# Expert weights of a two-block transformer kernel: one transfer with 8 KB runs for each matrix, in place of two with 4 KB runs

## The chip, the core and the metric

The kernel runs on one core of a Trainium2 chip. The metric is the device time of one execution in microseconds (us). The profile gives the engines the names PE (matrix multiplies), PEld (its weight loads), DVE (vector), ACT (scalar), POOL (GpSimd) and SP (the engine whose queue issues most transfers). A transfer is carried out by 16 DMA engines that all queues share.

## What is computed

Two transformer blocks work on 1024 tokens of width 1024 in float32. The first has an mLSTM and a convolution mixer and then a mixture of 64 experts, of which each token takes 8, plus a shared expert; the second has chunked attention and a state space branch and then 16 experts, of which each token takes 2. The change touches the experts alone. Cut to that, the reference is:

```python
def body(acc, xs):                       # for one block of rows of one expert e
    rows, rw, e = xs
    xb = hpad[rows]
    y = (jax.nn.silu(xb @ we_gate[e]) * (xb @ we_up[e])) @ we_down[e]
    return acc.at[rows].add(y * rw[:, None].astype(y.dtype)), None
...
shared = (jax.nn.silu(hf @ ws_gate) * (hf @ ws_up)) @ ws_down
```

An expert has three float32 matrices of 1 MB: gate and up, 1024 x 256, and down, 256 x 1024. The 80 experts of both blocks have 240 such matrices.

## The kernel before

The class `Moe` serves both blocks. Experts are ordered by their number of tokens and every rank has a fixed capacity (`CAPS1`: 400 down to 64 rows, `CAPS2`: 240 down to 64). A unit is an expert, or half of one with over 256 rows; the units of many rows (over 128) and of few rows alternate.

For each unit, `fetch` gathers the rows of its tokens into `xg` with an indirect transfer from POOL's queue (L1097), `trans` transposes them on PE, and `load` brings the three matrices of the expert with plain transfers from SP's queue (L1132, in `halves`). `split` turns every float32 half matrix into a high and a low part in float32r: ACT copies (L83, `guh`, `wdh`), DVE subtracts (L84, `gul`, `wdl`). PE multiplies three products of parts (`pg` for gate and up, `psy` for down). ACT scales the result into a tile `y` (L1268), of which there are three, and POOL issues an indirect transfer that adds the rows of `y` to `acc` in HBM (L1269, L1220 for experts of 64 rows), up to 128 rows each. I call it the scatter. Scatters of one block of the network add into the same tensor, so the program has each wait until the one before it has landed.

The loop `main` works on three units at once: in pass i it loads and gathers ahead, splits the gate, up and down matrices of unit i + 1, runs the gate and up matmuls of unit i, and the down matmuls and the scatter of unit i - 1. SP's queue keeps the order of the program; the other engines' order is chosen by a scheduler. The split parts have six places of a half matrix for gate and up, and three for down (`wd=3`), which is one and a half experts.

A loaded half matrix lies in a place `raw` of 4 KB per partition. There are eight, 4 MB in all, and a load waits for the split that reads the place's old content; a place that comes free is taken by the next load in SP's order. At the start of the first expert stage three places more are lent from a pool that is closed soon after (`Z = 3`); the shared expert's first matrices and, at the end, seven rows of tokens for the next stage (`head`) use the same places.

```python
    def halves(self, src):
        kc = src.shape[1]
        out = []
        for j in range(2):
            raw = self.tile("raw", [128, kc // 2, 2048 // kc], F32)
            self.k.nc.sync.dma_start(raw, src[:, j * kc // 2:(j + 1) * kc // 2])
            out.append(raw)
        return out
```

Of the kernel before, what the change touches and what calls it, by code (L numbers as in the profile page):

```python
# [7 lines left out]
F32 = mybir.dt.float32  # L8
# [21 lines left out]
class Kern:  # L30
# [793 lines left out]
    def moe1(self, es0, caps, es1, head):  # L824

        nc, I = self.nc, self.I
        dve, act, gp = nc.vector, nc.scalar, nc.gpsimd
        acc = self.acc_d = self.dram.tile([1024, 1024], F32, name="acc1")
        with ExitStack() as es:
            kp = self.pool(es1, "m1k")  # L830
            moe = Moe(self, "m1", 64, caps, I['we_gate'][0], I['we_up'][0], I['we_down'][0], self.h2_d, acc)
            moe.psum(es)
            moe.pools(self.pool(es1, "m1r"), raw=8)
            moe.pools(self.pool(es, "m1a"), gu=4)
            moe.pools(self.pool(es, "m1x"), x=1, sg=2)
            up = moe.shared_up(self.hT, I['ws_gate'][0], I['ws_up'][0], self.chain)

            def fill(n):
                for _ in range(n):
                    next(up, None)  # L840
            fill(FILL[0])
            with ExitStack() as e1, self.tc.manual_schedule(engines={mybir.EngineType.PE}):
                tp = self.pool(e1, "m1t")
                pl = self.logits(moe.pst, "pt")
                S = tp.tile([128, 8, 64], F32, name="S")
                act.activation(S, pl, AF.Sigmoid)
                br = tp.tile([128, 64], F32, name="br")
                b = I['b_router']
                nc.sync.dma_start(br, bass.AP(tensor=b.tensor, offset=b.offset, ap=[[0, 128], [1, 64]]))
                sel = tp.tile([128, 8, 64], F32, name="sel")  # L850
                dve.tensor_tensor(sel, S, br[:, None].to_broadcast([128, 8, 64]), op=OP.add)
                rep = tp.tile([128, 8, 64], F32, name="rep")
                m8 = tp.tile([128, 8, 8], F32, name="m8")
                for c in range(8):
                    dve.max(m8[:, c], sel[:, c])
                    dve.match_replace(rep[:, c], m8[:, c], sel[:, c], -3.0e38)
                mask = tp.tile([128, 8, 64], BF, name="mask")
                dve.tensor_tensor(mask, rep, sel, op=OP.not_equal)
                fill(FILL[1])
                wt = tp.tile([128, 8, 64], F32, name="wt")  # L860

                def gate():
                    dve.tensor_mul(wt, S, mask)
                    sm = tp.tile([128, 8], F32, name="sm")
                    dve.reduce_sum(sm, wt, axis=AX.X)
                    dve.reciprocal(sm, sm)
                    dve.tensor_scalar(sm, sm, 2.5, None, op0=OP.mult)
                    dve.tensor_tensor(wt, wt, sm[:, :, None].to_broadcast([128, 8, 64]), op=OP.mult)
                    return wt
                moe.setup(kp, mask, gate, fill)  # L870
            moe.pools(self.pool(es, "m1b"), xg=4, oh=2, q=2)
            with moe.ordered():
                with ExitStack() as e1:

                    raw = moe.room['raw']
                    moe.pools(self.pool(e1, "m1z"), raw=Z)
                    moe.room['raw'] = raw[:4] + raw[8:] + raw[4:8]
                    moe.start()
                    moe.split(0, 0)
                    moe.room['raw'] = raw[:8]  # L880
                fill(16)
                es0.close()
                mc = self.pool(es, "m1c", side="right")
                moe.pools(mc, gu=2, wd=3, su=2, hh=2, hl=2, y=3)
                moe.pools(self.pool(es, "m1y", side="right"), x=1)
                moe.room['gu'] = [moe.room['gu'][i] for i in GUO]
                moe.shared_down(I['ws_down'][0])
                moe.main()
                head([moe.tile("raw", [128, 4, 256], F32).rearrange("p a b -> p (a b)") for _ in range(7)], moe.pst)

            raw[:] = [(mc, 2, "gu" + n) for n in "hl"]
            moe.room['gu'] = moe.room['gu'][:2]
            moe.overflow()


class Moe:
# [228 lines left out]
        return [self.halves(w[ds(e, 1)].rearrange("o (p c) n -> p (o c) n", p=128)) for w in (self.wg, self.wu, self.wd)]  # L1125

    def halves(self, src):
        kc = src.shape[1]
        out = []
        for j in range(2):  # L1130
            raw = self.tile("raw", [128, kc // 2, 2048 // kc], F32)
            self.k.nc.sync.dma_start(raw, src[:, j * kc // 2:(j + 1) * kc // 2])  # L1132
            out.append(raw)
        return out

    def shared(self, w):

# [144 lines left out]
    def shared_up(self, hT, wg, wu, chain):  # L1282

        nc, behind = self.k.nc, self.k.tc.issue_after
        sq, ad, tr, sc = chain
        part = lambda v: v.rearrange("p a b -> p (a b)").rearrange("p (c n) -> p c n", n=128)
        raw, W = [], []
        for f in range(2):
            for w in (wg, wu):
                raw.append(part(self.tile("raw", [128, 4, 256], F32)))  # L1290
                nc.sync.dma_start(raw[-1], w[:, f * 128:f * 128 + 128].rearrange("(c p) n -> p c n", p=128))
        for j, r in enumerate(raw):
            h, l = (part(self.tile("gu", [128, 4, 256], F32R, "gu" + n)) for n in "hl")
            with behind(sq) if j > 1 else ExitStack(), behind(ad) if j > 1 else ExitStack():
                self.k.split(h, l, r)
            W.append((h, l))
        hs = self.hs = self.tile("x", [128, 2, 2, 1024], F32R)
        n = 0
        for f in range(2):
            for t in range(2):  # L1300
                c = slice(t * 512, t * 512 + 512)
                pg, pu = (self.psg.tile([128, 512], F32, name="pg") for _ in range(2))
                for p, (wh, wl) in zip((pg, pu), W[2 * f:]):
                    for i in range(8):
                        if i % 4 == 0:
                            if n:
                                yield
                            n += 1
                        with behind(sc) if n > 4 else ExitStack():
                            self.k.mm3(p, wh[:, i], wl[:, i], hT[0][:, i, c], hT[1][:, i, c], i == 0, i == 7)  # L1310
                s = self.tile("sg", [128, 512], F32)
                nc.scalar.activation(s, pg, AF.Sigmoid)
                nc.vector.tensor_mul(s, s, pg)
                nc.vector.tensor_mul(s, s, pu)
                self.k.split(hs[:, 0, f, c], hs[:, 1, f, c], s)
        yield
# [414 lines left out]
class Second:  # L1731
# [382 lines left out]
    def experts(self, em, hT, caps):  # L2114
        k, nc, I = self.k, self.k.nc, self.k.I
        dve, act, gp = nc.vector, nc.scalar, nc.gpsimd
        with ExitStack() as es:
            kp = k.pool(es, "m2k", side="right")
            moe = Moe(k, "m2", 16, caps, I['w_e_gate_2'][0], I['w_e_up_2'][0], I['w_e_down_2'][0], self.h3_d, self.acc_d)
            moe.psum(es)  # L2120
            with ExitStack() as e1:
# [4 lines left out]
                for o, n, nm in ((0, 4, 'group_bias_2'), (4, 16, 'expert_bias_2')):  # L2126
                    b = I[nm]
# [12 lines left out]
                e4, oh, p4 = T("e4", [8, 4]), T("goh", [8, 4]), T("p4", [8, 4])  # L2140
# [37 lines left out]
                    return wt.rearrange("p c g e -> p c (g e)")  # L2178
                moe.setup(kp, mask.rearrange("p c g e -> p c (g e)"), gate)
            em.close()  # L2180
            moe.pools(k.pool(es, "m2w"), raw=8, gu=6, wd=3, x=2, xg=4, oh=2, q=2, sg=2, su=2, hh=2, hl=2, y=3)
            with moe.ordered():
                moe.start()
                moe.main()
# [1 line left out]


FILL = 5, 2, 1, 1
Z = 3
GUO = 0, 0, 4, 4, 0, 0  # L2190

CAPS1 = [400] + [256] * 2 + [240] + [224] * 2 + [208] * 2 + [192] * 5 + [176] * 5 + [160] * 5 + [144] * 6 + [128] * 7 + [112] * 10 + [96] * 3 + [80] * 7 + [64] * 8
# [69 lines left out]
```

## Time and profile before

| what | value |
|---|---|
| device time, median of 3 runs | 2698.14 us (2696.0 to 2704.96) |
| device time of the profiled execution | 2692.12 us |
| span of its instructions | 2690.3 us |
| mean granted clock of TensorE | 0.963 of full speed |
| first expert stage | about 602 to 1566 us of the span |
| second expert stage | about 2421 to 2690 us |

The span runs from the first to the last instruction; 1.8 us lie around it. The profiled execution is one execution, 6.0 us below the median of the runs. In the views, "busy" is the time in which an engine executes instructions. A matmul's end is modelled, so a busy PE is not PE at its peak. An idle time is put down to the semaphore that came last by the profile; where the engine it names had long been done, it was another one, often a transfer.

### The profile page before, as it was taken

How to read it: one execution, taken by the hardware profiler on the slowest of the kernel's cores; microseconds unless marked ns; L12 is line 12 of the kernel's file. 1: busy time of each engine (PE TensorE's matmuls, PEld its weight loads, DVE VectorE, ACT ScalarE, POOL GpSimd, SP SyncE). 2: the span in 40 equal slices, each digit the busy share in tenths (PEclk: the TensorE clock that was granted, in tenths of full speed). 3: DMA queues.
4: the chain of work that ended last, by engine and by line, in shares of the span. 5: the costliest groups of instructions: out<-in, count | busy, mean ns of one | idle time of the engine just before them, and what ended most of it. 6: DMA issues, size and time to landing. Idle time of an engine off the chain costs nothing. (4 is left out here: it accounts for less than half of the span.)

```text
span 2690.3 us, 46156 instructions
## 1 busy us (share of the span) xinstructions
PE 2492.9 (93%) x17156; PEld 2127.8 (79%) x17156; DVE 1793.0 (67%) x4037; ACT 1332.8 (50%) x2327; POOL 534.0 (20%) x467
## 2 busy tenths in 40 slices
PE   6999987999999999999999939899999989987996
PEld 4798866987988888888877628688898778976884
DVE  4874788677777788887865453763243876278882
ACT  4322156324677776767765544223222772225773
POOL 0000021311232233233233230230001200002332
PEclk9999998999999999999999969999999999997998
DMA  7111183237899999999999864444311024148995
GB/s 252 33 50 61 44 279 113 103 109 268 244 308 309 312 314 299 307 316 315 301 319 317 252 216 95 123 89 107 114 32 56 1 95 150 56 165 291 320 291 120
DMA packets 259820, 507.52 MB, mean 189 GB/s; under 512 B 68761, under 2 KB 151905, under 8 KB 259592
## 3 DMA queue, kind: packets, MB, share of 16 engines
q1 hardware_dynamic: 231720, 409.36, 45.4%
q0 software_dynamic: 26720, 90.98, 14.9%
q10 hardware_dynamic: 1152, 4.19, 0.4%
q8 instruction: 136, 2.23, 0.3%
q14 instruction: 92, 0.75, 0.1%
HBM read 414.42 MB, written 90.04 MB: 188 GB/s over the span
## 5 line engine op out<-in xcount | busy, mean ns | idle before, releaser
L84 DVE TENSOR_TENSOR gul<-raw,guh 128x1024 fp32r<-128x1024 f32 x288 | 348.4, 1219 | 114.5 <-ACT guh L83 113.4
L83 ACT ACTIVATE guh<-raw 128x1024 fp32r<-128x1024 f32 x288 | 303.1, 1061 | 176.4 <-DMA raw<-in_we_gate_dram 67.8
L1185 PE MATMUL pg<-x,guh 128*128 128x320 f32 (+8 forms) x1248 | 383.7, 371 | 2.6 <-DVE sg L1233 2.6
L1184 PE MATMUL pg<-x,gul 128*128 128x160 f32 (+8 forms) x1092 | 278.1, 256 | 0.0
L1185 PEld LDWEIGHTS pg<-x,guh 128*128 128x128 f32 x1248 | 245.2, 200 | 9.9 <-DVE sg L1233 2.7
L1269 POOL DMA_INDIRECT acc<-y,m1idx x87 | 149.3, 1717 | 492.4 <-DMA acc<-y,m1idx 103.3
L1184 PEld LDWEIGHTS pg<-x,gul 128*128 128x128 f32 x1092 | 219.0, 201 | 3.4 <-issue 0.8
L84 DVE TENSOR_TENSOR wdl<-raw,wdh 128x1024 fp32r<-128x1024 f32 x144 | 175.6, 1222 | 60.9 <-ACT wdh L83 59.3
L88 PE MATMUL psy<-wdh,hh 128*128 128x512 f32 (+8 forms) x444 | 179.2, 405 | 7.4 <-ACT y L1268 7.0
L89 PE MATMUL psy<-wdl,hh 128*128 128x512 f32 (+8 forms) x444 | 175.4, 395 | 0.0
L90 PE MATMUL psy<-wdh,hl 128*128 128x512 f32 (+8 forms) x444 | 169.5, 400 | 0.0
L1097 POOL DMA_INDIRECT xg<-h_d,m1idx x95 | 122.4, 1289 | 180.7 <-PE pt L1119 91.9
L398 DVE SCALAR_TENSOR_TENSOR y<-u,cw,y 128x1024 f32<-128x1024 f32 x120 | 153.9, 1283 | 2.7
L83 ACT ACTIVATE wdh<-raw 128x1024 fp32r<-128x1024 f32 x144 | 151.6, 1054 | 7.3 <-PE psy L90 4.6
L88 PE MATMUL pg<-guh,x 128*112 128x256 f32 (+3 forms) x528 | 152.0, 288 | 1.0 <-ACT x L83 1.0
L1119 PEld LDWEIGHTS pt<-ident,xg 128*128 128x128 f32 (+8 forms) x888 | 119.3, 196 | 40.2 <-issue 18.6
L1119 PE MATMUL pt<-ident,xg 128*128 128x128 f32 (+8 forms) x888 | 134.2, 279 | 17.1 <-DVE x L84 5.3
L89 PE MATMUL pg<-gul,x 128*112 128x256 f32 (+3 forms) x528 | 149.9, 284 | 0.0
L90 PE MATMUL pg<-guh,x 128*112 128x256 f32 (+3 forms) x528 | 149.9, 285 | 0.0
L76 DVE TENSOR_TENSOR wlo<-wraw,whi 128x2048 fp32r<-128x2048 f32 (+2 forms) x37 | 83.3, 2251 | 92.9 <-ACT whi L75 92.8
L89 PE MATMUL pf<-bl,whi 128*128 128x512 f32 (+1 forms) x384 | 140.5, 369 | 3.0 <-DVE bl L1829 2.9
L88 PE MATMUL pf<-bh,whi 128*128 128x512 f32 (+1 forms) x384 | 139.3, 370 | 1.3 <-ACT g L1877 1.3
(906 smaller groups left out, 6972.9 us busy)
## 6 DMA issues: line engine op xcount, KB each, us to landing
raw<-in_we_gate_dram SPq DMA_DIRECT2D x128, 512.0 KB
raw<-in_we_up_dram SPq DMA_DIRECT2D x128, 512.0 KB
raw<-in_we_down_dram SPq DMA_DIRECT2D x128, 512.0 KB
wraw<-in_w_in_dram SPq DMA_DIRECT2D x26, 1024.0 KB
raw<-in_w_e_gate_dram SPq DMA_DIRECT2D x32, 512.0 KB
raw<-in_w_e_up_dram SPq DMA_DIRECT2D x32, 512.0 KB
raw<-in_w_e_down_dram SPq DMA_DIRECT2D x32, 512.0 KB
whi<-in_w_ada_dram SPq DMA_DIRECT2D x14, 1024.0 KB
```

Of the source, the lines that this page charges most:

```text
L76: (eng or nc.vector).tensor_sub(l, raw, h.bitcast(F32))
L83: self.nc.scalar.activation(hi, src, AF.Copy)
L84: self.nc.vector.tensor_sub(lo, src, hi.bitcast(F32))
L88: mm(out, ah, bh, start=first, stop=False)
L89: mm(out, ah, bl, start=False, stop=False)
L90: return mm(out, al, bh, start=False, stop=last)
L398: nc.vector.scalar_tensor_tensor(y, u[:, :, j:j + 64], cw[:, cc, j:j + 1], y, op0=OP.mult, op1=OP.add)
L1097: self.k.nc.gpsimd.indirect_dma_start(out=xg[:n], out_offset=None, in_=self.h_d[:, :], in_offset=bass.IndirectOffsetOnAxis(ap=idx[:n], axi ...
L1119: nc.tensor.transpose(pt[:, i, :n], xg[:n, 4 * j + i::8], k.ident[:n, :n])
L1184: mm(ps[:, 0], wl[:, q], x[:, i, 0, :m], start=False, stop=False)
L1185: mm(ps, wh[:, q], x[:, i, :, :m], start=i == 0, stop=i == 7)
L1269: nc.gpsimd.indirect_dma_start(out=self.acc_d[:, :], out_offset=bass.IndirectOffsetOnAxis(ap=idx[:n, b:b + 1], axis=0), in_=y[:n], in_offs ...
```

## The change

Each matrix is loaded by one transfer into one place of 8 KB per partition: the partition's 8 KB lie together in HBM for the routed experts, so a run is 8 KB in place of 4 KB. There are four such places in place of eight, again 4 MB. Both halves of a place are still split one after the other by two instructions; the place is free when both have been read. The lent places go from three of 4 KB to one of 8 KB. The shared expert's first four loads keep their size and lie in two places, and the seven rows of tokens at the end lie in halves of the four.

```diff
-            moe.pools(self.pool(es1, "m1r"), raw=8)
+            moe.pools(self.pool(es1, "m1r"), raw=4)
...
-                    moe.room['raw'] = raw[:4] + raw[8:] + raw[4:8]
+                    moe.room['raw'] = raw[:2] + raw[4:] + raw[2:4]
                     moe.start()
                     moe.split(0, 0)
-                    moe.room['raw'] = raw[:8]
+                    moe.room['raw'] = raw[:4]
...
-                head([moe.tile("raw", [128, 4, 256], F32).rearrange("p a b -> p (a b)") for _ in range(7)], moe.pst)
+                places = [moe.tile("raw", [128, 8, 256], F32).rearrange("p a b -> p (a b)") for _ in range(4)]
+                head([v[:, j:j + 1024] for v in places for j in (0, 1024)][:7], moe.pst)
...
     def halves(self, src):
+
         kc = src.shape[1]
-        out = []
-        for j in range(2):
-            raw = self.tile("raw", [128, kc // 2, 2048 // kc], F32)
-            self.k.nc.sync.dma_start(raw, src[:, j * kc // 2:(j + 1) * kc // 2])
-            out.append(raw)
-        return out
+        raw = self.tile("raw", [128, 8, 256], F32).rearrange("p a b -> p (a b)").rearrange("p (c n) -> p c n", c=kc)
+        self.k.nc.sync.dma_start(raw, src)
+        return [raw[:, j * kc // 2:(j + 1) * kc // 2] for j in range(2)]
...
         for f in range(2):
-            for w in (wg, wu):
-                raw.append(part(self.tile("raw", [128, 4, 256], F32)))
+            both = self.tile("raw", [128, 8, 256], F32)
+            for j, w in enumerate((wg, wu)):
+                raw.append(part(both[:, 4 * j:4 * j + 4]))
                 nc.sync.dma_start(raw[-1], w[:, f * 128:f * 128 + 128].rearrange("(c p) n -> p c n", p=128))
...
-            moe.pools(k.pool(es, "m2w"), raw=8, gu=6, wd=3, x=2, xg=4, oh=2, q=2, sg=2, su=2, hh=2, hl=2, y=3)
+            moe.pools(k.pool(es, "m2w"), raw=4, gu=6, wd=3, x=2, xg=4, oh=2, q=2, sg=2, su=2, hh=2, hl=2, y=3)
...
-Z = 3
+Z = 1
```

## Rows read from the trace of the kernel before

**Rows 1.** Stretches: length, busy PE PEld DVE ACT POOL, clock, DMA share, GB/s
```profile
800.00:900.00 100.00, 94.65 (x667) 85.55 (x666) 77.56 (x152) 71.25 (x110) 27.19 (x19) 0.97 1.01 312
900.00:1000.00 100.00, 100.00 (x668) 89.38 (x667) 79.41 (x141) 72.61 (x117) 33.49 (x21) 1.00 1.01 309
1400.00:1500.00 100.00, 98.09 (x674) 74.79 (x670) 55.22 (x122) 59.09 (x106) 30.62 (x23) 0.95 0.99 321
1500.00:1566.00 66.00, 43.38 (x265) 27.99 (x263) 19.67 (x33) 27.79 (x48) 16.08 (x10) 0.88 0.68 178
2500.00:2600.00 100.00, 100.00 (x715) 86.67 (x713) 80.39 (x163) 74.64 (x125) 33.14 (x24) 1.00 0.99 312
```

**Rows 2.** Waits from 640 to 1540 us: total us, times, longest
```profile
ACT guh L83 <- DMA raw<-in_we_gate_dram: 66.2, 37, 4.9
...
PE psy L88 <- ACT y L1268: 4.8, 6, 1.2
...
SPq L1132 <- DVE gul L84: 171.6, 106, 11.2
SPq L1132 <- DVE wdl L84: 136.5, 71, 11.6
```

**Rows 3.** Scatters from 700 to 1500 us: instructions, who waited, time to landing
```profile
L1269 POOL DMA_INDIRECT acc<-y,m1idx x79: 1326/1590/3154, 709.7 to 1494.5; - x79
L1220 POOL DMA_INDIRECT acc<-y,m1idx x4: 1583/1598/1907, 1410.3 to 1470.3; - x4
...
  ACT y L1268: 5.1, 2
...
DMA to landing us min/median/max: 5.2/8.9/11.5
```

**Rows 4.** Chain of work that ended last, end of the first expert stage: start, us
```profile
1550.50 6.10 DMA acc<-y,m1idx
...
1556.64 0.71 issue
1557.35 3.14 DMA acc<-y,m1idx
```

**Rows 5.** Scatters of the second expert stage, 2477 to 2640 us, and its last chain
```profile
L1269 POOL DMA_INDIRECT out_dram<-y,m2idx x18: 1336/1614/2292, 2477.6 to 2634.4; - x18
...
DMA to landing us min/median/max: 5.3/9.0/10.7
...
2665.19 6.49 DMA out_dram<-y,m2idx
```

**Rows 6.** DMA queues 700:1500, then 606:624, then 2025:2034: packets, MB, share
```profile
q1 hardware_dynamic: 49459, 180.07, 63.5%
q0 software_dynamic: 18672, 64.24, 35.2%
...
q1 hardware_dynamic: 1424, 5.16, 73.6%
...
q1 hardware_dynamic: 1040, 2.62, 78.1%
```

**Rows 7.** SP's issues of weights in two passes, in order of time
```profile
828.27 3.48 SPq L1132 DMA_DIRECT2D raw<-in_we_down_dram  x2
835.43 3.48 SPq L1132 DMA_DIRECT2D raw<-in_we_gate_dram  x2
841.86 1.93 SPq L1132 DMA_DIRECT2D raw<-in_we_up_dram  x2
```

**Rows 8.** ACT's splits of down matrices in the order of time
```profile
906.25 1.06 ACT L83 ACTIVATE wdh<-raw 128x1024 fp32r<-128x1024 f32 x1
...
921.58 1.05 ACT L83 ACTIVATE wdh<-raw 128x1024 fp32r<-128x1024 f32 x1
923.10 1.05 ACT L83 ACTIVATE wdh<-raw 128x1024 fp32r<-128x1024 f32 x1
```

**Rows 9.** Start of the first expert stage: SP's second expert, ACT's split of it
```profile
609.46 24.80 SPq L1132 DMA_DIRECT2D raw<-in_we_up_dram  x2
...
646.01 1.06 ACT L83 ACTIVATE guh<-raw 128x1024 fp32r<-128x1024 f32 x1 [1.18 <-PE pg L90]
```

**Rows 10.** The page: all DMA packets of the execution
```profile
DMA packets 259820, 507.52 MB, mean 189 GB/s; under 512 B 68761, under 2 KB 151905, under 8 KB 259592
```

## The prediction

> **What bounds the kernel now.** I read the stretches first. In both expert stages PE is busy 95 to 100% of the time, and the packets of the 16 DMA engines fill 0.99 to 1.01 of it [rows 1]. The reader is to see two resources that are full at once, so the second question is who really waits. The waits answer it for PE: its matmuls wait next to nothing, the longest entry is 4.8 us in 900, and none of it is for weights. ACT does wait for the gate matrix, 66.2 us in 37 of 64 experts, but that is idle time of an engine that is busy 59 to 73% [rows 1, 2]. SP waits for splits before almost every load: the places, and not the queue, set when a load is issued.
>
> The view that decides for me is that of the scatters. In 800 us there are 83, and one takes 8.9 us in the median from its issue to its landing; the next can be issued 0.71 us after that [rows 3, 4]. 83 x (8.9 + 0.71) = 798 us: the scatters are a chain that has no gap. The second stage has 18 of 9.0 us between 2477.6 and 2634.4 us, and 18 x 9.7 = 175 us are more than the 157 + 9 us that there are [rows 5], so that chain is full too (a median overstates it a little). Both stages end with the landing of such scatters [rows 4, 5]; PE is busy for only 43 of the first stage's last 66 us [rows 1]. That ACT waits for a scatter's landing only twice, 5.1 us in all [rows 3], says that the three `y` tiles still cover the lag. So PE and the chain of scatters are level, and the chain sets the ends.
>
> Why does a scatter take 8.9 us? With no weights in flight one of full size takes 6.10 or 6.49 us [rows 4, 5]. The 2.8 us above that are other packets on the same 16 engines, mostly weights: from 700 to 1500 us the loads take 63.5% of the engines' time, gathers and scatters 35.2% [rows 6]. The change works on this.
>
> **The change part by part.**
>
> *Packets.* 180.07 MB of loads are 43,960 packets of 4 KB (the rest of the count are a few bytes each) [rows 6], and 0.635 x 16 x 800 us = 8128 us make 185 ns for one; with only loads in flight it is 0.736 x 16 x 18 us over 1260 packets, 168 ns, and at 2.5 KB 0.781 x 16 x 9 us over 1023, 110 ns. The line through the last two is 13 ns and 38.7 ns per KB, so one packet of 8 KB would take 323 ns where two take 336. The trace has no load with 8 KB packets, so the saving lies between nothing (the packets are cut at 4 KB) and 13 ns for a pair. Over the 22,000 pairs from 700 to 1500 us that is at most 18 us of each engine's 800, 2.2%, or 0.2 us of the 9.6 us from one scatter to the next. I take the middle, 0.1 us per scatter.
>
> *Turns.* A full scatter is 128 rows, 8 packets on each engine. If each lets one weight packet go ahead, that costs 8 x 185 ns = 1.5 us now, about half of the 2.8 us seen. With packets of 8 KB and the same turns it is 8 x 357 ns = 2.9 us: up to 1.4 us more for each scatter. Nothing more is the other end: the weights need the same bytes in every pass, and what goes ahead of a scatter doesn't stand ahead of the next one. I take 0.3 us, near the lower end, since engines that are 99% booked can only trade places; what is lost is the time in which weights then are missing while a scatter is only being issued or confirmed. The Trainium skill (DMA: Bandwidth & Descriptors, "Queues, rings and completion order") states that each engine goes round its queues by whole packets. By that rule alone the sum would take the upper end, some 150 us; the trace agrees in that scatters beside weights take 8.9 us and not 6.1, but has packets of one size only.
>
> *Sum of the two.* 0.3 - 0.1 = 0.2 us for each scatter that has weights beside it: 89 of the first stage's 95 (the last six run after the weights) and 18 of the second's 25. 107 x 0.2 = 21 us, on the chains that end both stages.
>
> *Later loads.* Four places hold as much as eight did, but a place comes free with its second half. Now the halves of a matrix are issued 1.6 to 3.2 us apart (length of the pair less the last issue's 0.33 us) [rows 7]; after, the first half goes with or after the second one. A down matrix holds its place longest: its halves are split in neighbouring passes, as the pairs at 906 and 921 us show [rows 8], since `wd` has three places; its first 512 KB then lie about 15 us without use. So one half place in eight is lost on average, and ACT's first split of a gate waits for 1 MB: 1.7 us more (512 KB at some 310 GB/s), at most 64 x 1.7 = 109 us of ACT waiting. ACT's free 27% [rows 1], 243 us in 900, cover it, and PE uses the gate only a pass (15 us) later [rows 8]. I cost it at nothing; if that cover is gone it is the last rival.
>
> *The rest, at nothing.* SP issues 240 transfers fewer at a third of a microsecond, in a queue that waits for splits anyway [rows 2]. With one lent place, the second expert's up matrix goes as a whole when its second half went until now, at 633.9 us (24.80 us after 609.46, less the issue); it has 12 us until its split at 646.01 [rows 9], and 1 MB takes 3.5 us at 300 GB/s. The shared expert's loads and the token rows of the next stage keep their sizes; those rows are wanted only after the last scatters.
>
> *The time.* The profiled execution took 2692.1 us; 2692.1 + 21 = 2713.5. It lay 6.0 us under the median, so I forecast 2719 us for the runs.
>
> **The rivals.**
>
> *Nothing to measure.* The packets are still cut at 4 KB, or the queues share by bytes, and the later loads are covered. For it: ACT's and PE's slack above. Against it: nothing in the trace. The time is 2698, between 2690 and 2706.
>
> *Faster: the DMA engines get time back.* If a long packet costs the scatters no turn and saves its 13 ns, each of the 107 comes 0.2 us sooner, 21 us on the chains; PE, idle for 5 us or less in 100, then takes over as the bound, so I count 15: 2683. For it: a DMA share of 0.99 to 1.01, where every saved percent counts. It decides if the median landing falls under 8.9 us. The Trainium skill has a rule for this as well (the same page, "Rules for kernel authors": 1 MiB or more per transfer for bandwidth). By the page's estimate of 2.0 us plus bytes over 436 GB/s, two of 512 KB would take 6.4 us and one of 1 MB 4.4, 480 us less over 240 matrices; the trace differs, since loads overlap and the engines are never free between them.
>
> *Slower by late weights.* The gate's split is later by the 1.7 us and its second half starts only then, 1.1 us for ACT; where the passes are short the delay doesn't go away. The eight experts of 64 rows alternate with larger ones, 16 passes, and the second stage has eight small experts; 24 passes at 1.1 us are 26 us: 2724. For it: the gate is already just in time. Against it: PE waits for no weights now.
>
> **How the numbers follow.** My forecast gets 0.42; its own range is 2707 to 2745, from 0.1 to 0.45 us per scatter. Nothing to measure gets 0.28, faster 0.24, late weights 0.06. A change within 0.3% (8 us) can't be told from none here: the three runs themselves lie 9 us apart. Faster is then 0.24, the same 0.28 and slower 0.48. To hold the time 8 times in 10 the range must reach into the faster case, 2682, and to the end of the forecast's own, 2745; the 150 us of the upper bound are left out.
>
> **What would show it.** The step on packets: those under 8 KB fall from 259,592 [rows 10] by 61,440 (240 matrices of 256 packets), and 30,720 of 8 KB come in; if the count stays, the packets are cut. The step on turns: the median landing goes from 8.9 to about 9.1 us, and the first stage ends later than 1566. The step on loads: ACT's waits for the gate grow beyond 66 us, PE's for splits stay near zero. The prediction is wrong if scatters get quicker beside 8 KB packets, or if PE comes to wait for `guh` or `gul`.

## The result, and the profile after

The changed kernel takes 2734.19 us in the median of 4 runs (2721.43 to 2735.68), the kernel before 2697.07 us on the same chip (2693.08 to 2704.96). The ratio is 1.0131 with a 95% interval of 1.0101 to 1.0161: slower by 37 us. The forecast was 2719 us, within 2682 to 2745. The side and the range hold; the reason given does not.

The profiled execution took 2735.2 us, its span is 2733.4 us, 43.1 us more than before. About 4 us are there at the first load of an expert (602 us before, 607 after), and other kernels below with the same early part lie anywhere between 601 and 607, so these are not the change's. Between that and the last landing of the first expert stage lie 964 us before and 996 after, and the second stage's scatters take 204 and 210 us. So 32 and 6 us were lost inside the two expert stages. In the first the lag grows all along: 21 of the 32 us are there at the 73rd of 95 scatters, before the first expert of 64 rows.

The page's line on packets, as in [rows 10]:

```profile
DMA packets 225235, 507.43 MB, mean 186 GB/s; under 512 B 64905, under 2 KB 148049, under 8 KB 194296
```

Packets under 8 KB fell by 65,296, of which 3,856 are under 512 B: 61,440 are left, just what was forecast. There are 30,939 of 8 KB or more where there were 228. The packets are not cut.

The stretches, to be read against [rows 1], columns as there:

```profile
800.00:900.00 100.00, 97.96 (x708) 89.19 (x707) 79.28 (x152) 70.45 (x112) 28.75 (x20) 1.00 1.00 315
900.00:1000.00 100.00, 96.98 (x638) 84.93 (x638) 73.82 (x139) 65.63 (x107) 29.37 (x21) 1.00 0.98 301
1100.00:1200.00 100.00, 93.26 (x648) 79.98 (x647) 78.16 (x172) 66.19 (x108) 27.41 (x18) 0.93 0.91 281
...
1400.00:1500.00 100.00, 95.59 (x695) 69.06 (x692) 60.53 (x155) 59.08 (x104) 31.21 (x24) 0.98 0.95 306
1500.00:1566.00 66.00, 60.13 (x376) 45.69 (x376) 32.10 (x59) 38.32 (x69) 14.11 (x9) 0.95 0.86 275
...
2500.00:2600.00 100.00, 98.81 (x730) 87.60 (x729) 80.06 (x154) 72.80 (x124) 28.67 (x19) 1.00 0.93 294
```

The DMA engines, full before (0.97 to 1.01 in the stretches of 100 us from 800 to 1500), now have 2 to 9% free in most of them, and PE is idle for 1 to 7% (0 to 5% before). Longer turns of the weights' packets alone would leave the engines as full as ever. They are short of transfers that may start.

From the first load of an expert to the last down matmul of the first stage PE runs the same 6419 matmuls (before, then after, columns as above):

```profile
602.50:1546.90 944.40, 923.27 (x6419) 784.64 (x6417) 704.86 (x1483) 634.13 (x1029) 281.39 (x215) 0.99 0.96 298
606.90:1583.30 976.40, 935.11 (x6419) 791.99 (x6417) 702.82 (x1483) 626.87 (x1029) 272.38 (x215) 0.98 0.91 288
```

That is where the 32 us lie: from this matmul to the last landing it takes 19 us in both. PE is idle for 41.3 us where it was 21.1, and 11.8 us longer busy with the same work. Most of the second part is the clock: the trace has it at the lower of its two levels, 1.2 GHz, for 27 us before and 48 after, which by my estimate (21 us more at half the rate) is some 10 us. One such fall, at 1006.5 us, comes in PE's longest wait, 5.5 us for `sg`; how much of the lower clock follows from the waits wasn't tried.

The waits from 640 to 1540 us, against [rows 2]:

```profile
ACT guh L83 <- DMA raw<-in_we_gate_dram: 77.7, 32, 7.7
ACT y L1267 <- DMA acc<-y,m1idx: 20.9, 5, 6.3
ACT guh L83 <- DMA raw<-in_we_up_dram: 19.8, 14, 3.7
...
PE psy L88 <- ACT y L1267: 8.3, 7, 3.2
PE pg L1184 <- DVE sg L1232: 8.2, 4, 5.5
PE psy L88 <- ACT hh L83: 5.3, 4, 2.6
...
PE pg L1186 <- DVE gul L84: 1.2, 1, 1.2
...
SPq L1132 <- DVE gul L84: 158.7, 42, 7.2
SPq L1132 <- DVE wdl L84: 142.6, 42, 12.9
```

Two rows of the kernel before that [rows 2] doesn't have:

```profile
ACT guh L83 <- DMA raw<-in_we_up_dram: 10.1, 6, 2.8
...
PE pg L1185 <- DVE sg L1233: 2.6, 1, 2.6
```

ACT's wait for the gate grew by a sixth (to 90.4 us in a second trace of the changed kernel), and the wait for up doubled. PE still waits for split weights next to never (1.2 us for `gul`, 1.5 for `guh`). What PE waits for is ACT's and DVE's *other* results: `y`, `hh`, `sg`, 21.8 us in these three rows, where before it was 4.8 for `y` [rows 2], 2.6 for `sg` and nothing for `hh`. Over the whole stretch of the 6419 matmuls these waits are 30 us of PE's 41 idle ones, and were 11 of 21. The next view shows one of them.

The chain of work, one stretch of it (start us, us, what):

```profile
1107.61 2.35 DVE gul L84 x2
1109.99 8.64 DMA raw<-in_we_up_dram
1118.68 0.94 issue
1119.62 1.04 ACT guh L83
1120.88 0.59 ACT y L1267
1121.51 0.43 PE psy L88
```

and ACT and PE at its end on the timeline, with the idle time ahead of each and what ended it:

```profile
1118.65 2.00 ACT L83 ACTIVATE guh<-raw 128x1024 fp32r<-128x1024 f32 x2 [1.91 <-DMA raw<-in_we_up_dram]
...
1121.51 0.43 PE L88 MATMUL psy<-wdh,hh 128*48 128x512 f32 x1 [1.47 <-ACT y L1267]
```

A place is freed when DVE has split its second half (1109.96), SP issues the next load into it at once (1109.99), the load takes 8.64 us, ACT sits idle until it lands, splits both halves (2.00 us), and only then reaches a `y` that stands behind them in its queue; PE waits 1.47 us for that `y`. So in this pass late weights reach PE through ACT's order of work, not through a late `guh`. Of PE's 18 waits for `y`, `hh` or `sg` in that stretch, 13 (18 of the 30 us) end within 8 us after a wait of ACT for a load. That fits, but it doesn't show that the one caused the other in each case; the last two waits, 8 us together, have no such wait ahead of them.

The scatters from 700 to 1500 us, against [rows 3], and the chain at the end of the stage, against [rows 4]:

```profile
L1268 POOL DMA_INDIRECT acc<-y,m1idx x78: 1323/1580/2497, 702.0 to 1486.1; - x78
L1219 POOL DMA_INDIRECT acc<-y,m1idx x3: 1574/1598/1700, 1436.5 to 1493.2; - x3
```

```profile
1593.87 3.13 DMA acc<-y,m1idx
...
1597.76 4.90 DMA acc<-y,m1idx
```

81 where there were 83, and the stage ends at 1602.7 us, not 1566.2. When every issue in the trace is paired with the landing of its transfer, a scatter of this stretch takes 8.72 us in the mean (8.53 before; the medians are 8.8 and 8.9). Single scatters spread by 2.4 and 1.6 us (standard deviation), so the 0.2 us between the means has an uncertainty of 0.3: the forecast's +0.2 us per scatter is neither confirmed nor excluded. The experiments show that it isn't what sets the time.

### The profile page after: what moved, and what is told of

It is laid out like the page before. It is cut to its first block, busy times and chain, and to the rows that moved or that the text cites. A ratio compares the mean times of both kernels' runs of the same rounds, so it can differ in the third digit from the quotient of the medians.

```text
span 2733.4 us, 44990 instructions
## 1 busy us (share of the span) xinstructions
PE 2512.6 (92%) x17156; PEld 2142.5 (78%) x17156; DVE 1791.5 (66%) x4037; ACT 1322.3 (48%) x2327; POOL 530.0 (19%) x467
## 4 chain that ended last, share of the span: by engine, by line
PE 51%; DMA 17%; DVE 13%; ACT 6%; issue 3%; SPq 1%; POOL 0%; ACTq 0%; POOLq 0%; DVEq 0%
PE pf L88 6%; PE pf L89 6%; PE pf L90 6%; DMA raw<-in_we_gate_dram 6%; PE pg L1184 4%; DMA acc<-y,m1idx 3%; DVE gul L84 3%; DMA raw<-in_w_e_gate_dram 2%; PE psy L88 2%; PE psy L90 2%; PE psy L89 2%; PE pt L1120 2%; PE pg L1183 2%; PE py L90 2%; PE py L88 2%
## 5 line engine op out<-in xcount | busy, mean ns | idle before, releaser
L83 ACT ACTIVATE guh<-raw 128x1024 fp32r<-128x1024 f32 x288 | 291.6, 1054 | 157.6 <-DMA raw<-in_we_gate_dram 79.8
L1267 ACT ACTIVATE y<-psy,m1wsl 128x512 f32<-128x512 f32 (+8 forms) x174 | 116.4, 680 | 87.7 <-PE psy L90 44.6
L1120 PE MATMUL pt<-ident,xg 128*128 128x128 f32 (+8 forms) x888 | 139.1, 283 | 16.1 <-DVE x L84 8.3
L1098 POOL DMA_INDIRECT xg<-h_d,m1idx x95 | 115.9, 1220 | 160.9 <-PE pt L1120 75.2
```

Of the source, the lines that this page charges most:

```text
L83: self.nc.scalar.activation(hi, src, AF.Copy)
L1098: self.k.nc.gpsimd.indirect_dma_start(out=xg[:n], out_offset=None, in_=self.h_d[:, :], in_offset=bass.IndirectOffsetOnAxis(ap=idx[:n], axi ...
L1120: nc.tensor.transpose(pt[:, i, :n], xg[:n, 4 * j + i::8], k.ident[:n, :n])
L1267: nc.scalar.activation(y[:n, q], ps[:n], AF.Copy, scale=w[:n, b:b + 1])
```

## The experiments

Theory A is the prediction's: 8 KB packets make scatters longer, and the chain of scatters sets the time. Theory B: the places are at fault. A place of 8 KB comes free only with its second half, loads start later, and the engines run short of work. Times below stand against the kernel before in the same set of runs (2697.0 to 2699.4 us).

| kernel | us | ratio, 95% interval | matmuls, 640 to 1540 us | DMA share, GB/s | ACT `guh` waits for gate, up |
|---|---|---|---|---|---|
| before | 2697.1 | | 6187 | 0.98, 304 | 66.2, 10.1 |
| changed | 2734.2 | 1.0131 (1.0101 to 1.0161) | 6048 | 0.94, 296 | 77.7, 19.8 |
| four places, 4 KB packets | 2745.8 | 1.016 (1.0118 to 1.0202) | 5968 | 0.95, 292 | 128.6, 10.1 |
| seven places of 4 KB | 2731.7 | 1.0121 (1.0076 to 1.0167) | 5961 | 0.97, 293 | 130.8, 14.7 |
| eight places, 2 KB packets | 2698.9 | 0.9993 (0.9975 to 1.0011) | 6155 | 1.00, 303 | 84.5, 9.4 |
| by use, eight of 4 KB | 2705.5 | 1.0024 (1.0003 to 1.0046) | 6204 | 0.97, 304 | 0.9, 4.5 |
| by use, four of 8 KB | 2714.1 | 1.0073 (1.0047 to 1.0099) | 6159 | 0.95, 303 | 24.3, 16.5 |

**Four places, 4 KB packets.** In `halves` of the changed kernel:

```diff
-        self.k.nc.sync.dma_start(raw, src)
+        for j in range(2):
+            self.k.nc.sync.dma_start(raw[:, j * kc // 2:(j + 1) * kc // 2], src[:, j * kc // 2:(j + 1) * kc // 2])
```

> The changed kernel's four places of 8 KB, but each matrix is loaded by two transfers of 512 KB with 4 KB packets, one into each half of its place, issued back to back. What differs from the changed kernel is then the packet size alone; what differs from the kernel before is the places alone. Theory A (turns: 8 KB packets make the scatters longer): the time falls back to 2695 to 2705 us and the median landing of the scatters to 8.9 us. Theory B (places: a place comes free only with its second half, so loads are issued later and the engines idle): the time stays at 2725 to 2740 us, with a DMA share of 0.91 to 0.95 between 1100 and 1500 us as after the change. Both in part: between 2705 and 2725 us.

2745.84 us. With the packets of before and the places of after the loss is not gone, it is larger. Theory A falls as the cause; the places, with the order of work that is built around them, cost some 46 us.

**Seven places of 4 KB.** In the kernel before:

```diff
-            moe.pools(self.pool(es1, "m1r"), raw=8)
+            moe.pools(self.pool(es1, "m1r"), raw=7)
...
-            moe.pools(k.pool(es, "m2w"), raw=8, gu=6, wd=3, x=2, xg=4, oh=2, q=2, sg=2, su=2, hh=2, hl=2, y=3)
+            moe.pools(k.pool(es, "m2w"), raw=7, gu=6, wd=3, x=2, xg=4, oh=2, q=2, sg=2, su=2, hh=2, hl=2, y=3)
```

> The kernel before with seven places of 4 KB in place of eight, in both expert stages: the ring is one eighth shorter, packets and transfers stay. Theory A: no part of it touches the packets, so 2690 to 2710 us. Theory B: the down matrix's unused half place costs the changed kernel about one half place in eight on average, so this should cost about what the change costs, 2715 to 2745 us, with ACT waiting for the gate longer than 66.2 us.

2731.68 us, and ACT waits for the gate twice as long. One half place in eight, with no packet touched, costs 32 us, within theory B's range.

**2 KB packets.** In the kernel before:

```diff
-            self.k.nc.sync.dma_start(raw, src[:, j * kc // 2:(j + 1) * kc // 2])
+            v, s = (x.rearrange("p c n -> p (c n)").rearrange("p (c n) -> p c n", n=512) for x in (raw, src[:, j * kc // 2:(j + 1) * kc // 2]))
+            for q in range(2):
+                self.k.nc.sync.dma_start(v[:, q], s[:, q])
```

> The kernel before with its eight places of 4 KB, each half matrix loaded by two transfers with 2 KB runs per partition (four transfers of 256 KB for a matrix). Packets go the other way, places stay. Theory A: turns get shorter, so scatters land sooner than 8.9 us in the median, and the time is 2675 to 2695 us, unless the fixed 13 ns of a packet (four for two: 26 ns more for each pair of halves' packets) takes it back. Theory B: packets don't matter by themselves; 2695 to 2725 us, the rise being the packets' own cost of up to 3.5% of the engines' time.

2698.93 us, no change. Scatters take 8.35 us in the mean where they took 8.53, which is within the noise of the means. The 2675 to 2695 us of theory A are missed, and the interval leaves room for a gain of 7 us at most.

**Places of the down matrices' own.** In the changed kernel:

```diff
-            moe.pools(self.pool(es1, "m1r"), raw=4)
+            moe.pools(self.pool(es1, "m1r"), raw=3, rawd=2)
...
+        if kc == 2 and own:
+            out = [self.tile("rawd", [128, 1, 1024], F32) for _ in range(2)]
+            for j in range(2):
+                self.k.nc.sync.dma_start(out[j], src[:, j:j + 1])
+            return out
```

> The changed kernel with three places of 8 KB for gate and up (one transfer of 8 KB packets each) and two places of 4 KB that serve the down matrices alone (two transfers of 4 KB packets). The half of a down matrix that waits a pass for its split then holds back no half place that another matrix could use, and two thirds of the weights still come in 8 KB packets. Theory A: two thirds of the loss stay, 2718 to 2728 us. Theory B: if the unused half of the down matrix is what costs, most of the loss goes, 2695 to 2712 us; if any coarse place costs, the time stays above 2720 us.

2816.25 us (ratio 1.0426, 1.0385 to 1.0467), far above both ranges; theory B's second case, "above 2720 us", had no upper end and gains nothing from it. SP's waits from 640 to 1540 us:

```profile
SPq L1134 <- DVE wdl L84: 388.0, 50, 23.7
```

In [rows 2] that was 136.5. Places that only down may use make SP's queue stand, up to 23.7 us at a time, at a down load whose place is still held, and the next gate stands behind it. The run says how much a shared ring is worth in a queue that keeps its order; it doesn't isolate the down matrix's idle half, for which it was made.

**Two sums.** The scatters go in turn to two arrays, in the kernel before and in the changed one; the sum of the two is left out:

```diff
+        self.two = [acc_d, k.dram.tile([1024, 1024], F32, name=tag + "other")]
...
+            self.two.reverse()
-            nc.gpsimd.indirect_dma_start(out=self.acc_d[:, :], out_offset=bass.IndirectOffsetOnAxis(ap=idx[:n, b:b + 1], axis=0),
+            nc.gpsimd.indirect_dma_start(out=self.two[0][:, :], out_offset=bass.IndirectOffsetOnAxis(ap=idx[:n, b:b + 1], axis=0),
```

> The kernel before, its scatters going in turn to the accumulator and to a second array of the same shape, so that a scatter waits for the last but one and not for the last. It leaves out the sum of the two arrays, and the rows that go to the second one. Theory A as predicted (the chain of scatters is level with PE and sets the ends): the chain's 0.71 us from landing to issue goes and two scatters overlap, so the first stage loses the 15.7 us between its last ready y and its last landing and more, and the time falls to 2650 to 2675 us. Theory B (the places set the pace, the chain of scatters only follows): only part of the drain at the ends of the two stages is saved, 2680 to 2692 us.

> The same edit in the changed kernel (the same work is left out). Theory A (8 KB packets cost through the chain of scatters): without the chain the two kernels are equal, within 8 us of the kernel before with the same edit. Theory B (places): the distance stays, 27 to 45 us above the kernel before with the same edit, at 2710 to 2728 us.

2670.98 us (ratio 0.9899, 0.9869 to 0.993) and 2697.85 us (ratio 1.0, 0.998 to 1.002). For the kernel before, the prediction's reading holds at the ends: a looser chain gives 26 us, and in the first stage 13 of the 17.5 us won there come after the last down matmul, from which the last landing is 19 us away with one sum and 6 with two. Between 640 and 1540 us PE gets no further without the chain's wait (6207 matmuls, 6187 before). For the change the reading doesn't hold: with two sums 26.9 us of the 37 are still there, just under the 27 to 45 of theory B, whose 2680 to 2692 and 2710 to 2728 us are both missed. The other 10 us may go through the chain, but the intervals of the three ratios leave that open.

**Nine places, and its control.** A ninth place needs the room of one gathered block, so the control has three of these in place of four:

```diff
-            self.fetch(i + 4)
+            self.fetch(i + 3)
...
-                moe.pools(mc, gu=2, wd=3, su=2, hh=2, hl=2, y=3)
+                moe.pools(mc, raw=1, gu=2, wd=3, su=2, hh=2, hl=2, y=3)
```

(the first pair is the control's, both are in the kernel with nine places).

> The kernel before with three places for gathered token rows in place of four, and gathers issued three blocks ahead in place of four. A control for the next run, which needs their 4 KB. Gathers land in 9.2 us and a pass takes 15 us, so both theories expect 2690 to 2712 us.

> The control with a ninth place of 4 KB in both expert stages. Theory A: packets and turns are as before, so no change against the control. Theory B: a place fewer cost 32 us; PE waits little with eight, so a place more gives less, 5 to 20 us below the control, with ACT waiting for the gate less than the 66.2 us of before.

2757.13 us (ratio 1.0204, 1.0171 to 1.0238) and 2751.12 us (1.0184, 1.0162 to 1.0206). The control is itself 60 us slower, against both theories: its first load of an expert comes 16 us later (619 us, 602 before), and PE now waits for gathers, for which it waited 2.1 us before:

```profile
PE pt L1119 <- DMA xg<-h_d,m1idx: 55.2, 8, 16.1
```

The ninth place gives 6 us against it, with intervals that overlap. The pair settles nothing about places.

**Loads in the order of use.** No place is added; the down matrix is loaded later, between the next expert's gate and up, since its halves are split a pass after them. The calls that split it move to the same point in `main`. In the kernel before (half by half) and in the changed one (as a whole):

```diff
-            if r not in self.W:
-                self.W[r] = self.weights(self.k.nc.sync.value_load(self.eid[0:1, r:r + 1], min_val=0, max_val=self.E - 1))
+            new = r not in self.W
+            if new:
+                e = self.k.nc.sync.value_load(self.eid[0:1, r:r + 1], min_val=0, max_val=self.E - 1)
+                self.W[r] = [self.halves(self.of(self.wg, e)), None, []]
+                self.at[r] = e
+        self.late(i - 2, 2)
+        self.late(i - 1, 1)
+        if i < len(self.units) and new:
+            self.W[r][1] = self.halves(self.of(self.wu, e))
...
+            self.split_down(i - 1, 2)
+            self.split_down(i, 1)
...
-            self.split(i + 1, 2)
```

> The kernel before (eight places of 4 KB, 4 KB packets) with the loads issued in the order in which the halves are split: gate of the next expert, second down half of the expert before, first down half of this one, then up of the next. A down half is then loaded 1.3 passes ahead like all others and doesn't lie a pass or more without use. Theory B (places): as if places had been added; the gate comes some 5 us earlier, ACT's 66.2 us of waiting for it go below 40 us, and the time is 2670 to 2692 us. If the chain of scatters and PE are the bound instead, as predicted, no change: 2690 to 2705 us.

> The changed kernel (four places of 8 KB, one transfer of 8 KB packets) with the down matrix issued between the next expert's gate and up. A place is still freed by the second half, and a down matrix still holds one for a pass, but it is loaded a pass later. Theory B: part of the loss comes back, 2700 to 2725 us. Theory A: the packets stay, so the time does, 2725 to 2740 us.

2705.5 us (ratio 1.0024) and 2714.14 us (1.0073). ACT's waits, the first fence with eight places, the second with four:

```profile
ACT y L1268 <- DMA acc<-y,m1idx: 33.1, 8, 8.5
...
ACT guh L83 <- DMA raw<-in_we_gate_dram: 0.9, 1, 0.9
```

```profile
ACT guh L83 <- DMA raw<-in_we_gate_dram: 24.3, 10, 4.9
ACT guh L83 <- DMA raw<-in_we_up_dram: 16.5, 10, 5.6
```

In the kernel before the 66.2 us of waiting for the gate all go, and the time doesn't fall: that is a miss for theory B as it was put. ACT now waits for scatters instead (33.1 us, 5.1 before), and PE for gathers (8.0 us, 2.1 before). So that wait of ACT was free, or the new order costs as much elsewhere. In the changed kernel 20 of the 37 us come back (16 by the ratios) with the same packets and the same places, as theory B expected: there the moment at which loads can start does hold the kernel up.

**Packets at equal places.** The changed kernel and the first experiment once more, on one chip:

> The changed kernel once more, beside the next run, so that 8 KB and 4 KB packets into the same four places are compared on one chip. Both theories: 2725 to 2740 us.

> The four places of 8 KB filled by two transfers with 4 KB packets, once more. If long packets cost the scatters turns, this is below the changed kernel, by 10 us or more; if a long packet only saves its fixed 13 ns a pair, it is above it, by 5 to 15 us, as the two single comparisons (2745.8 and 2734.2 us) say; if packets don't matter, the two are within 5 us.

2734.81 us (ratio 1.0139, 1.0115 to 1.0163) and 2749.78 us (1.0185, 1.0161 to 1.021). Into the same places one transfer with 8 KB packets is 15 us quicker than two with 4 KB (12 by the ratios; 11.7 and 8 in the first pair). The second of the two texts names this case, 5 to 15 us. The weights' queue from 700 to 1500 us (packets, MB, share), in the order 8 KB, 4 KB, and then 2 KB in the kernel with eight places:

```profile
q1 hardware_dynamic: 23618, 171.99, 59.4%
```

```profile
q1 hardware_dynamic: 46068, 167.75, 60.9%
```

```profile
q1 hardware_dynamic: 97328, 177.24, 66.2%
```

By the working of the prediction's step on packets (share x 16 x 800 us over the packets that the MB make), one of 8 KB takes 362 ns, two of 4 KB 381 (370 in the kernel before), four of 2 KB 392. A scatter takes 8.74 us in the mean beside the first and 8.54 beside the second, again with 0.3 us of uncertainty. Whatever the long packets cost the scatters, the kernel is faster with them.

## Why the prediction was right and wrong

**What bounds the kernel before: right at the ends.** Two sums gave 26 us, most of it after the last down matmul, so the chain of scatters set the ends of the stages. That it has no gap was read from the median of 8.9 us; by the mean of 8.53, 83 scatters and their 0.71 us make 767 of the 800 us. Without the chain's wait PE did no more between 640 and 1540 us, so there the chain follows, and doesn't set, the pace. ACT's wait for the gate was covered, as far as loads in the order of use can say.

**Packets: the size was right, the route was not.** A pair saves 19 ns at equal places, and 8 against the kernel before, where I had at most 13. At equal places the kernel gains 12 to 15 us (8 to 12 in the first pair), where I put in 0.1 us for each of 107 scatters, 11 us; the gain doesn't come through the scatters, though, which don't get shorter. The rule of the Trainium skill (DMA: Bandwidth & Descriptors, "Rules for kernel authors") that wants 1 MiB or more in a transfer agrees in sign at equal places; the measured gain is 15 us, not the 480 of the estimate, which that page fits to single transfers issued by GpSimd, while these come from SP and overlap.

**Turns: not what explains the loss.** In both pairs at equal places the scatters are 0.2 us longer beside 8 KB packets, the 0.3 less 0.1 of the forecast, but the uncertainty of each difference is 0.3 us, and with loads in the order of use the sign is the other (8.59 us beside 8 KB, 8.67 beside 4 KB). The sum put this on the path that ends the stages. At equal places the time falls by 15 us whatever the scatters do, and the first stage's loss lies ahead of its last down matmul, so the forecast's 21 us came from a term that doesn't explain it. With one packet of the profile in each turn, the prediction's estimate by the Trainium skill's rule of whole packets in turn (the same page, "Queues, rings and completion order") was 1.4 us more for each scatter; the runs show 0.2, no more than their noise.

**Later loads: this step failed.** The price of nothing was wrong: the four coarse places cost 46 to 52 us, and one place of 4 KB less costs 32. "So one half place in eight is lost on average" is then too little, or not all. I set 1.7 us of lateness at each gate against ACT's idle share of 27%, and PE's use a pass later. Neither is cover enough. ACT's instructions run in the order of its queue, so while it waits for a gate or an up it holds back a `y` or `hh` for which PE waits soon, as the chain at 1107 to 1122 us shows for one pass; and ACT's idle time is partly that very wait. How lateness then lasts is my reading, not shown by a run of its own: a place's next load starts only after its split, so a late split makes the next load late, and DMA engines that are 99% booked don't make it up.

**The sum.** Places +52 us (1.0185 of 2697.9 is 50, and the medians lie 51.9 apart), 8 KB packets -15 us: +37 us. These are differences of the same three kernels, so that they add up proves nothing; each stands by its own comparison. So the rival of late weights names the cause, and its place was wrong too: next to no wait for `guh` or `gul` on PE, no special 24 short passes, but the whole of both stages. That the forecast came within 15 us of the time, with the right side, is luck: a loss of some 50 us was put at nothing, the packets' gain was about right, and a term for turns that no run confirms filled part of the gap.

**The rest at nothing: not contradicted.** Fewer issues on SP, the lent place and the shared expert's loads were not tried by themselves; the lent place is part of what the places cost here.

**What stays open.** The order of ACT's work is a rival that no run rules out. The scheduler builds it anew for every kernel: of ACT's 2327 instructions, compared by tile and shape in the order of time, 1530 stand in the changed kernel where they stood before, 1598 with 4 KB packets into the same places, 1811 with seven places, 2099 with 2 KB packets. Part of each difference, the 15 us at equal places too, may come from that order and not from the time at which loads land; no kernel here keeps the order and changes the places. How the 52 us divide between the first half that is issued late and the down half that lies unused wasn't isolated. Whether the 15 us are the packets' own or the halved number of transfers wasn't either, since both change together. And the sum of ACT's waits for weights doesn't follow the time from kernel to kernel (97.5 us in the changed kernel, 138.7 with 4 KB packets, 11.7 us apart).

## What to carry to other kernels

Merging two transfers into one also merges their buffers: count when a buffer comes free, not only its bytes, and try the merged transfer and the coarser buffer apart. Here the one long transfer gave some 15 us and the coarser buffers took some 50. A busy share of 73% on ACT was no cover for its waits: look at what stands behind the waiting instruction in the queue and who wants it. And compare the order of each engine's instructions before a difference is put down to one cause.

No kernel tried here beats the one before. The 2671 us with two sums leave work out.

## What was unexpected in the hardware

- The cost of a weight packet beside gathers and scatters is nearly proportional to its bytes: 98 ns for 2 KB, 190 for 4 KB, 362 for 8 KB. Going from 4 KB to 2 KB with unchanged places changed the time by nothing measurable (ratio 0.9993).
- Gathers three blocks ahead in place of four cost 60 us, though one lands in 9.2 us in the median: 55.2 us are 8 waits of PE, the longest 16.1 us, and the first load comes 16 us later; why wasn't followed up.
